# A two-layer hybrid trunk on one core: residual by loading transfers, squares summed by TensorE, weight sums on VectorE, parked tiles loaded ahead

## The chip, the cores and the metric

The kernel runs on one core of one Trainium2 chip. The metric is the device time of one execution in microseconds; lower is better. A time is the median of several runs of one program. A core has TensorE (PE in the profile, with its weight loads listed as PEld), VectorE (DVE), ScalarE (ACT), GpSimd (POOL) and SyncE (SP), which issues most transfers. Each engine takes its own instructions in order; semaphores tie them together.

## The reference

Two residual layers over a stream x of 1024 tokens by 1024 features, all float32. Each layer does

```python
    for layer in range(DEPTH):
        h = rms_norm(x, norm_mix[layer])
        # layer 0: RG-LRU recurrent block; layer 1: forgetting attention
        y_mem = memory_group(xq, mem, norm_mem[layer], w_mem_kv[layer], ...)
        x = x + jnp.concatenate([y_mix, y_mem], axis=-1) @ w_out[layer]
        x = x + sqrelu_mlp(rms_norm(x, norm_mlp[layer]), w_mlp_in[layer], w_mlp_out[layer])
```

with `sqrelu_mlp(h, w1, w2) = square(relu(h @ w1)) @ w2` and a hidden width of 4096. `memory_group` attends from the tokens to 256 normalised memory tokens, whose keys and values are one product with `w_mem_kv`. `rms_norm` needs, for each token, the mean of squares over the 1024 features.

## The kernel before, in words

Everything is kept transposed: features on the 128 partitions, tokens along the row, in tiles of 128 x 512 (one chunk m of 128 features, one half h of the tokens). The SBUF holds 86 such slots, named `f` (float32) or `r` (the rounded type fp32r that TensorE reads); a pool object hands them out and takes them back. A float32 product is made of three fp32r matmuls: each operand is split into `hi` (ScalarE, copy with rounding) and `lo` (VectorE, subtraction), and hi·hi, hi·lo and lo·hi are summed in PSUM. Weights go the same way: SP loads a raw tile `wr` (L307), ScalarE makes `wh` (L311), VectorE makes `wl` (L312; GpSimd for a part of them). The eight PSUM banks carry the names "pj" (2), "s" (2), "pt" (3) and "o" (1).

The order of each engine's instructions is made when the program is built: Python generators emit the work, some of them woven together, and a scheduler that simulates the engines orders what is emitted by its own estimate of times.

The MLP of a layer is cut into eight groups g of 512 hidden features. Each group does a first product `mlp_z` (w1, then relu and square) and a second `mlp_out` (w2). Both use a Strassen-like scheme with seven block products instead of eight (keys b11, b21, t2, t3, t1, t4, b22), so sums of tiles and sums of weight blocks are needed besides. The weight sums of a w1 unit that start from "S2" are seven additions by GpSimd in `_wunit` (L349 twice, L350 twice, L354 at double width, L351 twice), for the w2 units likewise. A `mlp_out` has seven passes of 24 matmuls into four banks; `copies` (ScalarE, L990) takes a bank into a tile at the first half of a sum, `plus` (VectorE, L995) adds a bank to a tile at the second half.

The residual stream x lies in DRAM as `xs` ("xspill" in the profile). Groups 0 to 6 add their results to it with accumulating transfers that GpSimd issues (`send`, L1122). Group 7 does it otherwise: at the key t1 of its `mlp_z`, `acc_load` lets SP load all 16 tiles of `xs`; as a first half comes out, GpSimd adds it to the loaded tile (L1143, 12 per layer); VectorE adds the second half, and `sink` stores the tile, as the output or (layer 0) back to `xs` with squares and splits for the next layer.

The sums of squares for a norm are made by `sqacc`: ScalarE squares a tile (L432), GpSimd adds the square to a running tile `ss` (L438), and `norm_fin_g` lets TensorE sum over partitions with four one-column matmuls against a constant column `cD` (L372), one per 128 tokens.

Two ways of bringing work forward matter here. In the second layer `mlp_park` does the first two products of groups 0, 1 and (in `mlp`, as "wait") 2 early, stores four tiles per group to DRAM ("park"), and `mlp_z` loads them when the group comes (L1044, L1047) and puts two of them into PSUM by a matmul with the identity (L1049). And `kv(l)`, which loads, normalises and projects the memory tokens, is a generator that is advanced from outside: for the second layer at the end of group 7's `mlp_z` of the first, where it loads (L546), splits (L555, L556) and squares; its products (L379) use the banks in `TUNE["kvt"]`, "pj" for the second layer. The output projections are `outproj2` (first layer) and `outproj` (second layer, L894), which add the residual on VectorE (L911, L865) and call `sqacc`.

Of the kernel before, what the change touches and what calls it, by code (L numbers as in the profile page):

```python
# [19 lines left out]
P = 128  # L20
# [57 lines left out]
class Unit:  # L78
# [3 lines left out]
    def __init__(self, src, names, at):  # L82
        self.src, self.names, self.buf = src, names, {}
# [42 lines left out]
def chain(*gs):  # L126
# [5 lines left out]
    "kvt": ('pt', 'pj'),  # L132
# [42 lines left out]
class Builder:  # L175
# [4 lines left out]
    def __init__(self, ctx, tc, ins, out):  # L180
# [36 lines left out]
        self.parked = {}  # L217
        self.xg = [None, None]
# [120 lines left out]
    def _wunit(self, hi, lo, unit, what):  # L339
        G, V = self.nc.gpsimd, self.nc.vector  # L340
# [117 lines left out]
    def norm_fin_g(self, h, bcast, behind=None):  # L458
        nc = self.nc
        ss = self.ss[h]  # L460
        st = self.psum("o")
        for t in range(4):
            self.mm(st[:, t:t + 1], [(ss[:, t * P:(t + 1) * P], self.cD)], behind if t == 0 else None)
# [3 lines left out]
        self.F.put(ss)  # L467
# [73 lines left out]
    def kv(self, l):  # L541
        nc = self.nc
        raw = [self.F.get() for _ in range(4)]
        for i in range(4):
            for j in range(2):
                nc.sync.dma_start(raw[i][:, j * M:(j + 1) * M], self.ins["memT"][2 * i + j])  # L546
        ss = self.F.get()
        xs, rel = [], []
        for i in range(4):
            a, b = self.R.get(), self.R.get()  # L550
            rel += [a, b]
            for j in range(2):
                g = self.pc(f"gmem{l}", 2 * i + j)
                s = slice(j * M, (j + 1) * M)
                nc.scalar.activation(a[:, s], raw[i][:, s], AF.Copy, scale=g)  # L555
# [3 lines left out]
            nc.scalar.activation(sq[:, :H], raw[i][:, :H], AF.Square)  # L559
# [293 lines left out]
    def outproj(self, h, ks, src, dst, gain, last, banks=("pj",)):  # L853
        nc = self.nc
        for m in range(8):
# [10 lines left out]
            if last:  # L866
                self.sqacc(m, h, xv)
# [10 lines left out]
    def outproj2(self, h, k0, k1, src, gain, side):  # L878
# [25 lines left out]
        for m in range(8):  # L904
# [7 lines left out]
            self.sqacc(m, h, xv)  # L912
# [47 lines left out]
    def plan_unit(self, name, i, names=Unit.ALL):  # L960
        src = dict(zip(("a11", "a12", "a21", "a22"), self.ins[name][4 * i:4 * i + 4]))
        u = Unit(src, names, len(self.plan))
        self.plan += [(None, 1024, u, k) for k in names]

    def plan_mlp(self, l, parked, wait):
        for g in wait:
            self.plan_unit("w1", 8 * l + g, Unit.ALL[:2])
        for g in range(8):
            self.plan_unit("w1", 8 * l + g, Unit.ALL[2:] if g in parked + wait else Unit.ALL)
# [27 lines left out]
    def relu2(self, f, src, h):  # L997
        n = slice(0, H)
        self.nc.vector.scalar_tensor_tensor(f[:, n], src, 0.0, self.rsb[h][:, n], ALU.max, ALU.mult)  # L999
        self.nc.scalar.activation(f[:, n], f[:, n], AF.Square)  # L1000

    def mlp_park(self, g):
# [4 lines left out]
        d = self.parked[g] = self.dr.tile([4, P, H], F32, name=self.nm("park"))  # L1007

        def done(o, ps):
            c = self.F.get()  # L1010
            self.nc.sync.dma_start(d[o], t[o][:, n])
            self.nc.vector.tensor_tensor(c[:, n], t[o][:, n], ps, ALU.add)
            self.relu2(c, c[:, n], 0)
            self.nc.sync.dma_start(d[2 + o], c[:, n])
            self.F.put(t[o], c)

        yield from self.product([self.psum("pj") for _ in range(2)], b21, True, done)

    def mlp_z(self, l, g, hook):
# [20 lines left out]
        if g in self.parked:  # L1040
            d = self.parked.pop(g)
            for o in range(2):
                f = self.F.get()
                nc.sync.dma_start(f[:, n], d[o])  # L1044
                t.append(f)
                f = hz[o]["b11"] = self.F.get()
                nc.sync.dma_start(f[:, n], d[2 + o])  # L1047
# [55 lines left out]
    def mlp_out(self, l, g):  # L1103
# [21 lines left out]
        def sink(q, a, b):  # L1125
            f = self.acc.pop((q, a, b))
# [9 lines left out]
        def keep(a, b):  # L1136
            dst = []

            def first(q, ps):
                self.copies(dst)(q, ps)  # L1140
                if g == 7:
                    c = self.acc[(q, a, b)][:, n]
                    G.tensor_tensor(c, c, dst[q][:, n], ALU.add)  # L1143
                    self.F.put(dst[q])

            def then(q, ps):
                if g == 7:
                    self.plus(self.acc[(q, a, b)], ps)
                    sink(q, a, b)
                else:  # L1150
                    self.plus(dst[q], ps)
                    send(dst[q], q, a, b)
# [3 lines left out]
        def end(q, ps):  # L1156
            if g == 7:
                self.plus(self.acc[(q, 0, 1)], ps)
                sink(q, 0, 1)
# [17 lines left out]
    def mlp(self, l, wait, nxt=None):  # L1177
# [3 lines left out]
        def hook(key):  # L1181
# [550 lines left out]
```

## Time and profile before

| | us |
|---|---|
| time, median of 3 runs | 2159.27 |
| lowest and highest run | 2156.13, 2165.36 |
| the profiled execution, its own time | 2165.67 |
| its span in the trace | 2164.0 |
| TensorE busy | 2066.3 (95%) |
| VectorE busy | 1694.2 (78%) |
| ScalarE busy | 1138.6 (53%) |
| GpSimd busy | 936.8 (43%) |

The profile is of one execution. Times of instructions are microseconds from the span's start. A group of instructions has its line, engine, operation, and output <- inputs by the program's names; brackets give idle time of the engine just before and what ended it. Matmuls overlap one another, so that the busy time of TensorE says little about the pace; the number of matmuls in a stretch, divided by its length, says more, and the granted clock (1.00 is full) stands beside it.

The first MLP begins at about 340 us and ends at about 1010; the second runs from about 1500 to the end, with its parked groups 0 to 2 up to about 1700.

### The profile page before, as it was taken

The numbers are of one execution on the slowest core, as the hardware profiler recorded it, in microseconds if no ns is written. First come the engines' busy times: TensorE is split into PE (matmuls) and PEld (weight loads), VectorE is DVE, ScalarE is ACT, GpSimd is POOL, SyncE is SP. The second block draws the span as 40 slices with busy tenths as digits, with TensorE's granted clock in tenths as the row PEclk, the third lists the DMA queues.
The fourth block names the chain that finished last, engine by engine and source line by source line (L and its number), as shares of the span: only waits on it lengthen the run. The fifth ranks groups of instructions, "written<-read, shape, count | busy, mean of one in ns | idle before, by whom it ended". The sixth has DMA issues, their size and how long they took to land.

```text
span 2164.0 us, 29751 instructions
## 1 busy us (share of the span) xinstructions
PE 2066.3 (95%) x10290; PEld 1713.5 (79%) x10290; DVE 1694.2 (78%) x2698; ACT 1138.6 (53%) x2154; POOL 936.8 (43%) x875
## 2 busy tenths in 40 slices
PE   8999997999999999987999999998989999999998
PEld 6898875777778778766998998776767777787786
DVE  8987689886886877878677778778857678768877
ACT  6765645544444544456555647566444444544443
POOL 3213324444444535547342333424463544445445
PEclk9999999999999999998999999999999999999999
DMA  6323352347436446544768446945263474474482
GB/s 204 119 79 107 113 185 73 84 82 156 88 84 140 95 89 129 124 129 166 268 232 288 131 142 219 288 145 169 83 146 98 107 148 89 79 152 93 87 210 78
DMA packets 126103, 297.38 MB, mean 137 GB/s; under 512 B 14144, under 2 KB 16256, under 8 KB 125952
## 3 DMA queue, kind: packets, MB, share of 16 engines
q1 hardware_dynamic: 84480, 211.50, 29.0%
q0 software_dynamic: 41472, 83.97, 21.9%
q8 instruction: 81, 1.33, 0.2%
q14 instruction: 70, 0.57, 0.1%
HBM read 186.27 MB, written 109.15 MB: 137 GB/s over the span
## 4 chain that ended last, share of the span: by engine, by line
PE 45%; DVE 16%; issue 8%; DMA 5%; POOL 3%; ACT 3%; SPq 0%; DVEq 0%; POOLq 0%; ACTq 0%
PE pspt L979 13%; PE pspj L379 10%; PE pss L979 10%; PE pspj L979 7%; DVE wl L312 4%; DVE r L452 3%; DVE f L999 2%; DMA xspill<-f 2%; DVE f L995 1%; PE pso L979 1%; PE pss L1360 1%; PE pspt L1402 1%; DMA wr<-in_w_dram 1%; POOL wr L354 1%; DVE f L1084 1%
## 5 line engine op out<-in xcount | busy, mean ns | idle before, releaser
L312 DVE TENSOR_TENSOR wl<-wr,wh 128x1024 fp32r<-128x1024 f32 (+2 forms) x362 | 446.6, 1244 | 98.7 <-ACT wh L311 96.0
L979 PE MATMUL pspt<-r,wh 128*128 128x512 f32 x1552 | 494.4, 400 | 3.8 <-ACT f L990 2.2
L1122 POOL DMA_DIRECT2D xspill<-f x224 | 292.2, 1990 | 301.2 <-DVE f L995 292.0
L311 ACT ACTIVATE wh<-wr 128x1024 fp32r<-128x1024 f32 (+3 forms) x411 | 305.4, 765 | 122.4 <-PE pss L979 26.7
L979 PEld LDWEIGHTS pspt<-r,wh 128*128 128x128 f32 x1552 | 294.5, 190 | 77.5 <-issue 2.7
L979 PE MATMUL pss<-r,wh 128*128 128x512 f32 x1024 | 328.9, 400 | 14.4 <-DVE r L452 10.9
L452 DVE TENSOR_TENSOR r<-f,r 128x512 fp32r<-128x512 f32 x282 | 240.7, 865 | 113.3 <-DMA xspill<-f 50.5
L979 PE MATMUL pspt<-r,wl 128*128 128x512 f32 x776 | 309.7, 400 | 2.1 <-DVE wl L312 2.1
L379 PE MATMUL pspj<-wh,r 128*128 128x256 f32 (+1 forms) x1408 | 273.0, 288 | 15.8 <-DVE f L995 11.6
L979 PE MATMUL pspj<-r,wh 128*128 128x512 f32 x816 | 264.5, 405 | 12.4 <-DVE f L865 4.6
L979 PEld LDWEIGHTS pss<-r,wh 128*128 128x128 f32 x1024 | 194.0, 190 | 68.8 <-DVE r L452 17.5
L449 ACT ACTIVATE r<-f 128x512 fp32r<-128x512 f32 x282 | 172.6, 626 | 135.0 <-DMA xspill<-f 51.5
L379 PEld LDWEIGHTS pspj<-wh,r 128*128 128x128 f32 x1408 | 223.6, 191 | 18.9 <-issue 11.9
L1000 ACT ACTIVATE f<-f 128x512 f32<-128x512 f32 x128 | 80.9, 632 | 275.0 <-DVE f L999 274.9
L349 POOL TENSOR_TENSOR wr<-wr,wr 128x512 f32<-128x512 f32 x64 | 104.4, 1817 | 266.1 <-DVE wl L312 252.5
L979 PE MATMUL pss<-r,wl 128*128 128x512 f32 x512 | 204.1, 399 | 4.6 <-DVE wl L312 4.6
L379 PE MATMUL pspj<-wl,r 128*128 128x256 f32 (+1 forms) x704 | 201.6, 287 | 1.2 <-DVE wl L312 1.1
L979 PEld LDWEIGHTS pspj<-r,wh 128*128 128x128 f32 x816 | 155.6, 192 | 52.3 <-ACT wh L311 5.4
L379 PE MATMUL pspj<-r,wh 128*128 128x512 f32 x528 | 175.0, 407 | 10.0 <-ACT wh L311 5.7
L979 PEld LDWEIGHTS pspt<-r,wl 128*128 128x128 f32 x776 | 148.7, 192 | 39.4 <-DVE wl L312 3.8
L979 PE MATMUL pspj<-r,wl 128*128 128x512 f32 x408 | 161.3, 401 | 1.0 <-DVE wl L312 0.9
L351 POOL TENSOR_TENSOR wr<-wr,f 128x512 f32<-128x512 f32 x64 | 146.5, 2582 | 14.9 <-issue 14.6
(291 smaller groups left out, 3985.8 us busy)
## 6 DMA issues: line engine op xcount, KB each, us to landing
wr<-in_w_dram SPq DMA_DIRECT2D x134, 512.0 KB, 4.3
xspill<-f POOLq DMA_DIRECT2D x224, 256.0 KB, 6.7
f<-xspill SPq DMA_DIRECT2D x104, 256.0 KB, 5.0
xspill<-f SPq DMA_DIRECT2D x64, 256.0 KB, 3.2
f<-in_xT_dram SPq DMA_DIRECT2D x32, 256.0 KB, 3.4
wr<-in_wkv_dram SPq DMA_DIRECT2D x16, 512.0 KB, 3.6
wr<-in_wina_dram SPq DMA_DIRECT2D x15, 512.0 KB, 3.7
wsp<-wh SPq DMA_DIRECT2D x14, 512.0 KB, 4.7
```

The costliest lines, as they stand in the source:

```text
L311: self.wact = self.nc.scalar.activation(hi, raw, AF.Copy)
L312: eng.tensor_tensor(lo, raw, hi.bitcast(F32), ALU.subtract)
L349: G.tensor_tensor(r["a11"][:, d], r["a11"][:, d], r["a21"][:, d], ALU.subtract)
L351: G.tensor_tensor(r["a12"][:, d], r["a12"][:, d], x, ALU.subtract)
L354: G.tensor_tensor(r["a21"], r["a21"], r["a22"], ALU.add)
L379: self.lastmm = self.nc.tensor.matmul(out, lhsT=a, rhs=b, start=(j == 0), stop=(j == n - 1))
L449: i = self.nc.scalar.activation(hi[:, :n], src, AF.Copy)
L452: self.nc.vector.tensor_tensor(lo[:, :n], src, hi[:, :n].bitcast(F32), ALU.subtract)
L979: self.lastmm = self.nc.tensor.matmul(ps, lhsT=a, rhs=b, start=(start and c == 0 and j == 0), stop=(c == n - 1 and j == 2), skip_group_che ...
L999: self.nc.vector.scalar_tensor_tensor(f[:, n], src, 0.0, self.rsb[h][:, n], ALU.max, ALU.mult)
L1000: self.nc.scalar.activation(f[:, n], f[:, n], AF.Square)
L1122: nc.gpsimd.dma_start(self.xs[2 * q + a, :, b * H:(b + 1) * H], f[:, n], accum_op=ALU.add)
```

## The change

Six things are written otherwise.

1. In group 7, the residual tile is added by a transfer: GpSimd issues an accumulating load from `xs` onto the tile that holds the first half (after the change L1180, 12 per layer). `acc_load` and its 16 loads go; the last four tiles are loaded by SP in the middle of `mlp_out`.
2. In `outproj2` and in the second layer's last `outproj`, `sq_pe` replaces `sqacc`: each square tile goes to TensorE as four one-column matmuls that add up in a bank "o" (after the change L456), held back by two chunks; GpSimd's additions go.
3. The weight sums of group 0's w1 unit are made by VectorE, in both layers (`u.dve`).
4. Parked tiles of group 0 stay in SBUF; those of groups 1 and 2 are stored, and loaded in the middle of the preceding group's `mlp_out` (`mlp_back`), four transfers each.
5. The second layer's memory tokens are loaded from group 7's key t2 on, and split from its key b22 on, ordered behind the last relu square (`lastsq`). Their products use "pt" banks. The norm steps in group 0 come at t2 and t3.
6. The second layer's last `outproj` uses the banks "pj", "s" and "pt" instead of "pj" alone.

```diff
@@ TUNE
-    "kvt": ('pt', 'pj'),
+    "kvt": ('pt', 'pt'),
@@ _wunit
-        G, V = self.nc.gpsimd, self.nc.vector
+        V = self.nc.vector
+        G = V if unit.dve else self.nc.gpsimd
@@ new
+    def sq_pe(self, m, h, xt):
+        sq = self.F.get()
+        self.nc.scalar.activation(sq[:, :H], xt, AF.Square)
+        if m == 0:
+            self.stp[h] = self.psum("o"), []
+        self.stp[h][1].append((m, sq))
+        self.sq_mm(h, 2)
+
+    def sq_mm(self, h, keep):
+        st, todo = self.stp[h]
+        while len(todo) > keep:
+            m, sq = todo.pop(0)
+            for t in range(4):
+                self.nc.tensor.matmul(st[:, t:t + 1], lhsT=sq[:, t * P:(t + 1) * P], rhs=self.cD,
+                                      start=(m == 0 and t == 0), stop=(m == 7), skip_group_check=True)
+            self.F.put(sq)
@@ norm_fin_g
+        if h in self.stp:
+            self.sq_mm(h, 0)
+            st, ss = self.stp.pop(h)[0], None
+        else:
...
@@ kv
                 nc.sync.dma_start(raw[i][:, j * M:(j + 1) * M], self.ins["memT"][2 * i + j])
+        yield
+        behind = self.lastsq if l else None
...
@@ outproj
-                self.sqacc(m, h, xv)
+                (self.sqacc if gain is None else self.sq_pe)(m, h, xv)
@@ outproj2
-            self.sqacc(m, h, xv)
+            self.sq_pe(m, h, xv)
@@ plan_mlp
+            u = self.plan_unit("w1", 8 * l + g, Unit.ALL[2:] if g in parked + wait else Unit.ALL)
+            u.dve = g == 0
@@ new
+    def mlp_back(self, g):
+        if g in self.parked:
+            d = self.parked[g]
+            self.parked[g] = [self.F.get() for _ in range(4)]
+            for i, f in enumerate(self.parked[g]):
+                self.nc.sync.dma_start(f[:, :H], d[i])
@@ mlp_out
-    def acc_load(self):
-        self.acc = {(q, a, b): self.load_x(2 * q + a, b, self.xs)
-                    for a, b in ((0, 0), (1, 0), (1, 1), (0, 1)) for q in range(4)}
...
             def first(q, ps):
                 self.copies(dst)(q, ps)
                 if g == 7:
-                    c = self.acc[(q, a, b)][:, n]
-                    G.tensor_tensor(c, c, dst[q][:, n], ALU.add)
-                    self.F.put(dst[q])
+                    nc.gpsimd.dma_start(dst[q][:, n], self.xs[2 * q + a, :, b * H:(b + 1) * H], accum_op=ALU.add)
...
         yield from run([self.psum(k) for k in more], "b21", True, c11[1], "t3")
+        mid()
         yield from run(A, "t2", False, c21[0], "t1")
         C = [self.psum(k) for k in more]
+        acc = [self.load_x(2 * q, 1, self.xs) for q in range(4)] if g == 7 else None
...
@@ mlp
+        def hook7(key):
+            if key in ("t2", "b22") and nxt is not None:
+                advance(nxt)
...
-            drain(self.mlp_out(l, g))
+            drain(self.mlp_out(l, g, lambda: self.mlp_back(g + 1)))
@@ run
-        drain(self.outproj(1, K_X, self.xs, self.xs, "gmlp1", True))
+        drain(self.outproj(1, K_X, self.xs, self.xs, "gmlp1", True, ("pj", "s", "pt")))
```

How the instructions move, at three places. First GpSimd at the end of the first layer's MLP, before the change (L1143 adds a loaded residual tile and a first half; L438 adds squares for the next norm):

```order
L1143 TENSOR_TENSOR f_829_7854<-f_829_7854,f_875_8102 128x512
...
L438 TENSOR_TENSOR f_880_8127<-f_880_8127,f_889_8171 128x512
L1143 TENSOR_TENSOR f_830_7856<-f_830_7856,f_896_8194 128x512
L1143 TENSOR_TENSOR f_831_7858<-f_831_7858,f_897_8203 128x512
L1143 TENSOR_TENSOR f_832_7860<-f_832_7860,f_898_8212 128x512
```

and after it (L591 adds the squares of the memory tokens, L440 is the former L438):

```order
L591 TENSOR_TENSOR f_834_7956<-f_834_7956,f_845_7988 128x512
L1180 DMA f_856_8064<-xspill 128x512
L1180 DMA f_857_8073<-xspill 128x512
...
L440 TENSOR_TENSOR f_864_8116<-f_864_8116,f_873_8160 128x512
L1180 DMA f_880_8183<-xspill 128x512
L1180 DMA f_881_8192<-xspill 128x512
```

Each of the additions is a transfer now, at the same place in GpSimd's queue, and the memory tokens' squares come ahead of the first four.

Second, VectorE at the entry of the first MLP after the change (L351, L352, L356 and L353 are the weight sums, L313 the `wl` of a weight, L941 and L471 a residual addition and a split of the projection):

```order
L351 TENSOR_TENSOR wr_69<-wr_69,wr_71 128x512 x2
L463 SCALAR_TENSOR_TENSOR r_406_3789<-f_329_3342,par,r_405_3788 128x512
L313 TENSOR_TENSOR wl_76<-wr_70,wh_73 128x1024
L941 TENSOR_TENSOR f_368_3554<-f_368_3554,pspj_3556 128x512
L463 SCALAR_TENSOR_TENSOR r_408_3793<-f_345_3416,par,r_407_3792 128x512
L352 TENSOR_TENSOR f_383_3627<-wr_72,wr_69 128x512
L471 TENSOR_TENSOR r_398_3723<-f_347_3441,r_397_3722 128x512
...
L356 TENSOR_TENSOR wr_71<-wr_71,wr_72 128x1024
...
L353 TENSOR_TENSOR wr_70<-wr_70,f_383_3627 128x512
```

Before, these additions stood in GpSimd's queue, mixed with the last squares; now they stand between VectorE's splits and residual additions.

Third, TensorE in the second layer's last output projection after the change (L381 are the projection's matmuls, L456 the squares' with one column):

```order
L381 MATMUL pspt_15021<-r_1578_14954,wl_77 128x512
L456 MATMUL pso_14978<-cD,f_1581_14976 128x1 x4
L381 MATMUL pspj_15048<-r_1356_13394,wh_75 128x512
L381 MATMUL pspj_15048<-r_1357_13395,wh_75 128x512
L456 MATMUL pso_14978<-cD,f_1584_15000 128x1 x4
L456 MATMUL pso_14978<-cD,f_1591_15035 128x1 x4
L381 MATMUL pspj_15048<-r_1356_13394,wl_78 128x512
```

Before, one set of four such matmuls stood here in all, behind the last addition; now eight sets stand between the projection's matmuls, three of them close together at this place.

More of the change, by code (lines that the diff above doesn't have):

```diff
@@ L217, in __init__ @@
         self.parked = {}
+        self.stp = {}
         self.xg = [None, None]
@@ L459, in norm_fin_g @@
         nc = self.nc
[L460 to L463, printed above, removed]
+        if h in self.stp:
+            self.sq_mm(h, 0)
+            st, ss = self.stp.pop(h)[0], None
+        else:
+            ss = self.ss[h]
+            st = self.psum("o")
+            for t in range(4):
+                self.mm(st[:, t:t + 1], [(ss[:, t * P:(t + 1) * P], self.cD)], behind if t == 0 else None)
         self.vx[h] = self.small(4, f"vx{h}")
@@ L466, in norm_fin_g @@
         self.rs_tok[h] = self.rsqrt(self.vx[h], 4, f"rst{h}")
-        self.F.put(ss)
+        if ss is not None:
+            self.F.put(ss)
         if bcast:
@@ L554, in kv @@
                 s = slice(j * M, (j + 1) * M)
-                nc.scalar.activation(a[:, s], raw[i][:, s], AF.Copy, scale=g)
+                k = nc.scalar.activation(a[:, s], raw[i][:, s], AF.Copy, scale=g)
+                if behind is not None:
+                    self.after(k, behind)
                 nc.vector.scalar_tensor_tensor(b[:, s], raw[i][:, s], g, a[:, s].bitcast(F32), ALU.mult, ALU.subtract)
@@ L558, in kv @@
             sq = ss if i == 0 else self.F.get()
-            nc.scalar.activation(sq[:, :H], raw[i][:, :H], AF.Square)
+            k = nc.scalar.activation(sq[:, :H], raw[i][:, :H], AF.Square)
+            if behind is not None:
+                self.after(k, behind)
             if i:
@@ L963, in plan_unit @@
         self.plan += [(None, 1024, u, k) for k in names]
+        return u
     def plan_mlp(self, l, parked, wait):
@@ L1006, in mlp_park @@
         yield from self.product([self.psum("pj") for _ in range(2)], b11, True, self.copies(t))
-        d = self.parked[g] = self.dr.tile([4, P, H], F32, name=self.nm("park"))
+        kept = []
         def done(o, ps):
             c = self.F.get()
-            self.nc.sync.dma_start(d[o], t[o][:, n])
             self.nc.vector.tensor_tensor(c[:, n], t[o][:, n], ps, ALU.add)
             self.relu2(c, c[:, n], 0)
-            self.nc.sync.dma_start(d[2 + o], c[:, n])
-            self.F.put(t[o], c)
+            kept.append(c)
         yield from self.product([self.psum("pj") for _ in range(2)], b21, True, done)
+        kept = t + kept
+        if g:
+            d = self.dr.tile([4, P, H], F32, name=self.nm("park"))
+            for i, f in enumerate(kept):
+                self.nc.sync.dma_start(d[i], f[:, n])
+            self.F.put(*kept)
+            self.parked[g] = d
+        else:
+            self.parked[g] = kept
+    def mlp_back(self, g):
[4 more added lines that the diff above has]
+                self.nc.sync.dma_start(f[:, :H], d[i])
     def mlp_z(self, l, g, hook):
@@ L1157, in end @@
             if g == 7:
-                self.plus(self.acc[(q, 0, 1)], ps)
-                sink(q, 0, 1)
+                self.plus(acc[q], ps)
+                sink(acc[q], q, 0, 1)
             else:
```

37 lines of the change are left out of this document (13 added, 24 removed).

## The prediction

> **What bounds the kernel now.** I read the page's first section, then a table of windows, then TensorE's list of waits, and last the timeline where the waits lie.
>
> ```profile
> span 2164.0 us, 29751 instructions
> PE 2066.3 (95%) x10290; PEld 1713.5 (79%) x10290; DVE 1694.2 (78%) x2698; ACT 1138.6 (53%) x2154; POOL 936.8 (43%) x875
> ```
>
> TensorE (PE) is busy for 95% of the span, so all that any reordering can return lies in the other 5% and in stretches where it is busy at a lower clock. The next view has one row for each stretch: its bounds and length, the busy time and instruction count of PE, weight loads, VectorE (DVE), ScalarE (ACT) and GpSimd (POOL), TensorE's granted clock, and the DMA share and rate.
>
> ```profile
> 320.00:370.00 50.00, 37.52 (x145) 27.99 (x144) 50.00 (x55) 26.81 (x44) 26.21 (x14) 0.93 0.23 76
> 930.00:1000.00 70.00, 60.03 (x239) 46.38 (x238) 62.64 (x66) 41.50 (x76) 46.92 (x29) 0.95 0.35 118
> 1000.00:1020.00 20.00, 8.38 (x55) 8.19 (x54) 18.62 (x33) 10.46 (x24) 14.65 (x13) 0.66 0.53 180
> 1480.00:1550.00 70.00, 60.90 (x238) 45.63 (x237) 58.89 (x80) 37.91 (x62) 35.82 (x28) 0.90 0.56 180
> 1570.00:1580.00 10.00, 6.77 (x23) 5.13 (x22) 8.15 (x10) 6.07 (x11) 8.64 (x6) 0.83 0.28 64
> 1600.00:1620.00 20.00, 17.44 (x66) 13.10 (x65) 9.67 (x9) 6.02 (x9) 14.59 (x15) 0.91 0.93 174
> 1650.00:1700.00 50.00, 43.01 (x169) 32.46 (x168) 30.61 (x36) 21.19 (x35) 25.26 (x23) 0.93 0.69 150
> 1780.00:1840.00 60.00, 59.58 (x255) 47.45 (x254) 46.65 (x53) 27.93 (x44) 25.24 (x22) 1.00 0.43 91
> 2120.00:2140.00 20.00, 16.36 (x58) 12.42 (x57) 20.00 (x24) 12.02 (x20) 8.64 (x6) 0.83 0.13 52
> ```
>
> The row at 1780 is the calm middle of the second MLP: 255 matmuls in 60 us, 0.235 us each at clock 1.00; a pass of 24 is 5.65 us. Elsewhere the lost time is the length minus 0.235 times the count. Seam 1, entry of the first MLP (320 to 370): 50 − 34.1 = 15.9. Seam 2, its end (930 to 1020): 13.8 + 12.9 = 26.7. Seam 3, entry of the second MLP and its parked groups (four rows from 1480): 14.0 + 4.6 + 4.5 + 10.2 = 33.3. Seam 4, the end of the program: 6.4. Together 82 us lie at the places that the change touches. In 320 to 370 and 2120 to 2140 VectorE is busy for the whole stretch. Two lists of waits name the releasers (total us, times, longest).
>
> ```profile
> PE pspj L379 <- DVE f L995: 11.6, 1, 11.6
> PE pss L979 <- DVE r L452: 10.9, 15, 4.8
> PE pspt L1049 <- DMA f<-park: 6.7, 2, 4.1
> PE pss L979 <- DVE wl L312: 4.6, 1, 4.6
> ...
> ACT r L555 <- DMA f<-in_memT_dram: 8.8, 1, 8.8
> ```
>
> VectorE releases most of it, and parked tiles coming back release 6.7 us.
>
> **The change, part by part. Seam 1: weight sums and squares.** The timeline gives start, length, engine, operation and, in brackets, the idle time before it.
>
> ```profile
> 331.00 0.68 DVE L942 TENSOR_TENSOR f<-f,f 128x512 f32<-128x512 f32 x1
> 332.14 1.92 POOL L438 TENSOR_TENSOR f<-f,f 128x512 f32<-128x512 f32 x1 [5.33 <-ACT f L432]
> 332.81 1.79 DVE L949 SCALAR_TENSOR_TENSOR f<-f,par,f 128x512 f32<-128x512 f32 x1
> ...
> 344.88 5.24 POOL L349 TENSOR_TENSOR wr<-wr,wr 128x512 f32<-128x512 f32 x2 [4.35 <-DVE wl L312]
> 351.75 3.98 POOL L350 TENSOR_TENSOR f<-wr,wr 128x512 f32<-128x512 f32 x2
> 351.84 1.05 PE L372 MATMUL pso<-cD,f 128*128 128x1 f32 x8 [0.70 <-POOL f L438]
> 355.69 2.85 POOL L354 TENSOR_TENSOR wr<-wr,wr 128x1024 f32<-128x1024 f32 x1
> 358.50 3.39 POOL L351 TENSOR_TENSOR wr<-wr,f 128x512 f32<-128x512 f32 x2
> 364.30 0.50 PE L979 MATMUL pss<-r,wl 128*128 128x512 f32 x1 [4.61 <-DVE wl L312]
> ```
>
> A VectorE operation on two SBUF tiles takes 0.68 us at 331.00 and 1.79 beside a GpSimd addition: each GpSimd tensor operation here costs VectorE about 1.1 us. Seven square additions (L438) go: 7 × 1.1 = 7.7. The weight sums of group 0 keep GpSimd at work for 5.24 + 3.98 + 2.85 + 3.39 = 15.5 us; if VectorE does only such operations in it, it loses 15.5 × (1 − 0.68/1.79) = 9.6. On VectorE they cost it six operations of 0.68 and one of double width, 5.4, so 4.2 remain. Relief of VectorE: 11.9. TensorE pays: the row at 351.84 is one set of four one-column matmuls, 1.05 us; eight sets stand where one stood, 7 × 1.05 = 7.35. Net −4.6 if all relief reaches TensorE; I take −4. Bounds: all 15.9 return, −8.5; or only the 4.61 named at 364.30 goes, 7.35 − 4.61 = +3.
>
> The Trainium skill, "SBUF — State Buffer", section "Who interferes with whom", says that a VectorE operation with two SBUF inputs and a GpSimd operation that reads SBUF exclude each other for the whole instruction. By that rule seven additions like the one of 1.92 us would give back up to 13.4 instead of 7.7, and the seam would come to some −9. The row at 332.81 shows 1.1, and I stay with it.
>
> **Seam 2: the residual of the last group, and the early load of the second layer's memory tokens.**
>
> ```profile
> 968.89 0.64 PE L979 MATMUL pss<-r,wh 128*128 128x512 f32 x1 [4.75 <-DVE r L452]
> 985.29 12.80 POOL L1143 TENSOR_TENSOR f<-f,f 128x512 f32<-128x512 f32 x8
> 1013.19 0.55 PE L379 MATMUL pspj<-wh,r 128*128 128x256 f32 x1 [11.62 <-DVE f L995]
> ```
>
> Twelve additions (1.6 us each by the row at 985.29) and 12 of 16 loads go; 12 accumulating transfers come. Contention falls by 12 × 1.1 = 13 us on VectorE, but three square additions of the memory tokens and eight of their splits move into the stretch near 950 that was busy before, which takes back about 3 × 1.1 + 8 × 0.44 = 7 (0.44 is an estimate: half a 0.68 row for half the columns, and start-up). At 1013.19 the memory products wait 11.62 us for a "pj" bank that VectorE frees with its last additions; now they take "pt" banks, which the last pass does not use: freed one pass, 5.65 us, sooner, and VectorE gets there earlier. I take 8 of the 12.9 lost after 1000. ScalarE's 8.8 us on the late memory tokens goes too; it lay behind residual loads on SP's queue. Of the 13.8 lost before 1000 I take 6, the net relief. Seam 2: −14. Bounds: only the bank wait shrinks, −8; nearly all returns, −24.
>
> What the transfers cost is seen from the accumulating stores of groups 0 to 6: the same engine, size and kind, in the other direction (rows: of the page's issues; of one line, min/median/max).
>
> ```profile
> xspill<-f POOLq DMA_DIRECT2D x224, 256.0 KB, 6.7
> L1122 POOL DMA_DIRECT2D xspill<-f x224: 842/1631/4887, 407.5 to 2083.6; - x112
> DMA to landing us min/median/max: 3.7/6.7/12.8
> ```
>
> Issue 1.63 plus landing 6.7 plus VectorE's 0.68 is 9.0 us at the medians. VectorE's addition comes one pass after the copy and TensorE wants the bank another pass later, so 11.3 us are free: hidden. At the maxima it is 18.4, 7 us late; that is a rival below. The last four residual tiles still come through SP, issued three passes ahead: nothing.
>
> **Seam 3: squares, banks and parked tiles.**
>
> ```profile
> 1516.65 1.22 PE L979 MATMUL pspj<-r,wh 128*128 128x512 f32 x2 [4.26 <-DVE f L865]
> 1576.62 1.62 PE L979 MATMUL pspj<-r,wh 128*128 128x512 f32 x3 [3.23 <-ACT wh L311]
> 1609.76 1.10 PE L1049 MATMUL pspt<-f,ident 128*128 128x512 f32 x2 [2.56 <-DMA f<-park]
> ```
>
> The squares pay 7.35 again. Seven additions less and the weight sums moved relieve VectorE by 11.9 as at seam 1; seven banks instead of two let the output projection run while VectorE adds, so the 4.26 at 1516.65 should go. Of the 14.0 lost in 1480 to 1550 I take 10. Parked tiles of groups 1 and 2 are loaded in the preceding group's output passes, five of 5.65 us ahead of use; group 0's are never stored. The 6.7 us of waits go, with a little of the low clock behind them: 7. Net 7.35 − 17 = −10. Bounds: all but 2 returns, −24; only the park waits go, +1.
>
> **Seam 4** is seam 2's residual part without a next layer.
>
> ```profile
> 2122.02 5.09 POOL L1143 TENSOR_TENSOR f<-f,f 128x512 f32<-128x512 f32 x3 [2.98 <-ACT f L990]
> 2128.32 0.50 PE L979 MATMUL pss<-r,wh 128*128 128x512 f32 x1 [3.06 <-DVE r L452]
> ```
>
> Three visible additions slow VectorE just ahead of the 3.06 wait. I take −3 of 6.4, bounds 0 and −6.
>
> Sum: −4 − 14 − 10 − 3 = −31 (bounds −4 and −62). The profiled execution took 2165.67 us for its span of 2164.0, and lies 6.4 above the median 2159.27 of runs from 2156.13 to 2165.36. So 2134.7 for such an execution, and **2128** for the median.
>
> **The rivals.** (A) *VectorE stays the bound.* It is full for all of 320 to 370, takes the sums over, and gets the memory splits where it was late. Then each seam gives its lower end, +3 − 8 + 1 + 0 = −4: 2155. Against it: GpSimd's 15.5 us really leave those stretches. (B) *Nearly all lost time returns*, since stalls feed each other: a stall lowers the clock (0.66 to 0.83 in the windows), and late matmuls delay the next copies. Sum of the upper ends, −62: 2097. Against it: the waits have many releasers, and the change does not touch the weights' splits that end several. (C) *Slower: the squares' matmuls stop TensorE.* They stand in order among the projection's matmuls, and each set needs ScalarE's square of a tile that VectorE has just added. Where VectorE lags by more than the two chunks (11.3 us) that they are held back, all behind them waits. At 16 sets × 4.26 us (the wait on just such an addition, at 1516.65) that is +68, against −31: 2196. It decides from 31/16 = 1.9 us per set. Against it: 4.26 occurred at a lag of no chunks; for it: in the second layer two sets stand next to each other at two places, with less than two chunks ahead. (D) *The accumulating loads are late*: 7 us at the maxima, for two passes in each layer, is 28: 2156. For it: those transfers run where VectorE is busiest; against it: the median fits.
>
> The rule for (D) in the Trainium skill, the same page and section: a transfer issued by GpSimd that looks stalled by VectorE was starved of the port while its descriptors were written. The spread of L1122's issue, 0.84 to 4.89 us, agrees that issuing can stretch; by the rule (D) would be the likelier of the two no-change cases.
>
> **How the numbers follow.** Forecast 0.55 (own range 2112 to 2142), A 0.14, B 0.16, C 0.07, D 0.08. The range 2104 to 2157 leaves out about half of B, C, and the far halves of A and D: 0.2. Half a per cent, about what can be told from no change, is 10.8 us: faster is below 2148.5, slower above 2170. Faster: 0.55 + 0.16 + half of A + a little of D = 0.80. Slower: most of C, 0.06. Same: 0.14.
>
> **What would show it.** Right: the wait for L995 by the memory products falls to under 4 us; no wait for park is left; the lost time in the windows at the four seams falls from 82 to about 50, with sixteen sets of one-column matmuls of about 1.05 us included; VectorE's 512-wide operations near 350 read 0.68. Wrong: waits of several us ahead of the one-column matmuls (C), VectorE additions waiting for the accumulating transfers in the last groups (D), or a VectorE still full at both entries with TensorE waiting for wl (A).

## The result and the profile after

The changed kernel takes 2133.52 us (median of 4 runs, 2129.36 to 2142.39), the kernel before 2158.84 us in the 4 runs that stand with it (2156.13 to 2165.36): a ratio of 0.9884, 95% interval 0.9845 to 0.9922. The forecast was 2128, range 2104 to 2157. The profiled execution of the change took 2132.55 us for a span of 2130.8, 33.1 less than the profiled one of before; the medians differ by 25.3.

The first section of the page after:

```profile
span 2130.8 us, 29902 instructions
PE 2065.7 (97%) x10402; PEld 1716.9 (81%) x10402; DVE 1654.5 (78%) x2712; ACT 1137.0 (53%) x2154; POOL 857.8 (40%) x847
```

TensorE does 112 records more and is busy just as long. Its mean granted clock over the span is 0.989, where it was 0.981. As an estimate from these two, full clock was withheld for 1.9% of 2164.0 us, 41 us, before and for 1.1% of 2130.8, 23 us, after: up to 18 of the 33 us can be time at the low clock that no longer occurs. GpSimd has 79 us less to do.

To say where the time went, I took the start of the same VectorE instruction in two traces and looked at how the difference grows from place to place (us of the change's trace; a positive number is time that the other kernel takes more in that stretch). The first row is what the change saved; the other rows belong to the experiments below.

| stretch | 0–290 | 290–420 seam 1 | 420–860 | 860–1065 seam 2 | 1065–1415 | 1415–1720 seam 3 | 1720–2080 | 2080–end seam 4 |
|---|---|---|---|---|---|---|---|---|
| before | 3.8 | 11.0 | -0.2 | 7.2 | 0.9 | 4.5 | 0.5 | 5.3 |
| forecast of the saving | 0 | 4 | 0 | 14 | 0 | 10 | 0 | 3 |
| u_sq | 2.1 | 1.2 | 0.6 | -0.9 | 1.5 | -1.3 | 0.3 | 0.0 |
| u_s2 | 1.4 | -0.4 | -0.8 | -0.7 | 2.6 | 1.3 | -0.2 | 0.0 |
| u_sq_s2 | 0.8 | 10.3 | -0.3 | 0.3 | 2.1 | -2.2 | -0.3 | 0.0 |
| u_res | 5.5 | -1.1 | -0.5 | 2.3 | 1.6 | 0.4 | 0.2 | 4.3 |
| u_kvt | 0.0 | -1.6 | -0.6 | 0.7 | 0.5 | -3.9 | -0.2 | 0.0 |
| u_kv | 0.0 | -1.3 | -0.2 | -3.7 | 2.5 | -4.6 | -0.1 | 0.1 |
| u_kv_res | 6.9 | -1.2 | -0.5 | 8.2 | 1.1 | -1.5 | 0.0 | 4.4 |
| u_banks | 4.5 | 0.1 | 0.3 | -0.3 | -1.1 | -1.3 | -0.2 | 0.0 |
| u_park | 3.7 | -1.9 | 0.2 | -1.3 | 0.4 | 6.5 | -0.2 | 0.0 |
| k_mid | 6.9 | -2.2 | 0.2 | -1.5 | 3.0 | 1.3 | 0.1 | 0.0 |
| k_lull | 2.0 | -1.6 | 0.3 | -3.2 | 3.5 | -6.8 | 0.1 | 0.1 |
| k_best | 1.0 | -1.7 | -0.3 | -4.1 | 0.7 | -4.8 | -0.2 | 0.0 |

The four seams give 28.0 of the 33.0; the rest came in stretches that the change leaves as they were, and differs from run to run. The rows also show how far one execution can be trusted: where a kernel leaves a stretch as in the change, it still differs by up to 6.9 us before 290, from -2.2 to +0.1 at seam 1, from -1.3 to +0.3 at seam 2, by up to 3.5 between the seams 2 and 3, by nothing to speak of at seam 4, and from -6.8 to +1.3 at seam 3. So a few us at seam 3 mean nothing in one execution.

The table of windows of the change, with the columns of the prediction's:

```profile
320.00:370.00 50.00, 50.00 (x240) 41.17 (x239) 43.26 (x72) 30.26 (x48) 5.55 (x7) 1.00 0.28 90
```
```profile
940.00:950.00 10.00, 5.90 (x22) 3.90 (x22) 10.00 (x18) 8.39 (x15) 4.58 (x5) 0.94 0.64 104
950.00:960.00 10.00, 7.63 (x18) 5.40 (x19) 10.00 (x13) 7.04 (x12) 5.88 (x5) 0.55 0.52 160
...
970.00:980.00 10.00, 9.49 (x42) 7.37 (x41) 3.40 (x6) 2.20 (x5) 2.65 (x5) 1.00 1.07 239
...
990.00:1000.00 10.00, 7.16 (x46) 6.75 (x45) 9.99 (x12) 5.49 (x15) 9.11 (x8) 0.83 0.62 220
```
```profile
1440.00:1480.00 40.00, 36.53 (x174) 29.07 (x174) 26.14 (x62) 22.76 (x53) 11.07 (x18) 0.85 0.34 105
1480.00:1520.00 40.00, 36.86 (x163) 29.38 (x162) 32.91 (x57) 22.58 (x36) 4.50 (x8) 0.90 0.45 135
```

At the entry of the first MLP TensorE is busy for all 50 us at clock 1.00 and VectorE has 7 us to spare, where it had none. At the end of the first layer a hole is left: only 40 matmuls in the 20 us from 940, at a clock of 0.55 in its second half, while VectorE is full. The waits of TensorE, and one of VectorE:

```profile
PE pspj L381 <- ACT wh L312: 7.6, 3, 5.5
PE pspt L1011 <- DVE f L1027: 6.1, 3, 4.2
PE pss L1011 <- DVE r L471: 5.1, 14, 1.2
PE pss L1011 <- ACT f L1022: 4.5, 3, 2.3
...
DVE f L1027 <- DMA f<-xspill: 11.7, 6, 6.0
```

The first row lies in the first 100 us and stood there before (7.4). The waits of 11.6 (memory products for a bank), 6.7 (parked tiles) and 4.6 us (weights' wl) are gone. New is the last row: VectorE waits for the accumulating loads.

### The profile page after: what moved, and what is told of

It reads as the page before. It is cut to its first block, busy times and chain, and to the rows that moved or that the text cites. A ratio compares the mean times of both kernels' runs of the same rounds, so it can differ in the third digit from the quotient of the medians.

```text
span 2130.8 us, 29902 instructions
## 1 busy us (share of the span) xinstructions
PE 2065.7 (97%) x10402; PEld 1716.9 (81%) x10402; DVE 1654.5 (78%) x2712; ACT 1137.0 (53%) x2154; POOL 857.8 (40%) x847
## 4 chain that ended last, share of the span: by engine, by line
PE 55%; DVE 13%; issue 6%; DMA 4%; ACT 1%; POOL 1%; DVEq 0%; SPq 0%; POOLq 0%; ACTq 0%
PE pspt L1011 15%; PE pss L1011 12%; PE pspj L381 10%; PE pspj L1011 8%; DVE wl L313 3%; DVE r L471 3%; DVE f L1031 2%; DMA xspill<-f 2%; PE pso L1011 2%; PE pspt L381 1%; PE pspt L1438 1%; PE pss L1396 1%; DMA f<-xspill 1%; DVE f L1027 1%; DVE f L1130 1%
## 5 line engine op out<-in xcount | busy, mean ns | idle before, releaser
L313 DVE TENSOR_TENSOR wl<-wr,wh 128x1024 fp32r<-128x1024 f32 (+2 forms) x362 | 442.2, 1232 | 112.6 <-ACT wh L312 108.0
L471 DVE TENSOR_TENSOR r<-f,r 128x512 fp32r<-128x512 f32 x282 | 225.0, 808 | 100.3 <-DMA xspill<-f 57.6
L1011 PE MATMUL pspj<-r,wh 128*128 128x512 f32 x816 | 259.3, 397 | 4.1 <-ACT f L1022 1.8
L381 PE MATMUL pspj<-wh,r 128*128 128x256 f32 (+1 forms) x1280 | 246.7, 286 | 3.9 <-ACT wh L312 1.7
L381 PEld LDWEIGHTS pspj<-wh,r 128*128 128x128 f32 x1280 | 200.9, 188 | 7.0 <-ACT wh L312 1.9
L351 POOL TENSOR_TENSOR wr<-wr,wr 128x512 f32<-128x512 f32 x60 | 94.6, 1777 | 271.6 <-DVE wl L313 258.8
L381 PE MATMUL pspj<-wl,r 128*128 128x256 f32 (+1 forms) x640 | 181.5, 284 | 1.2 <-DVE wl L313 1.1
L381 PE MATMUL pspj<-r,wh 128*128 128x512 f32 x488 | 163.7, 411 | 9.6 <-ACT wh L312 5.9
L353 POOL TENSOR_TENSOR wr<-wr,f 128x512 f32<-128x512 f32 x60 | 140.2, 2650 | 17.8 <-issue 17.6
```

Source lines behind the costliest of these rows:

```text
L313: eng.tensor_tensor(lo, raw, hi.bitcast(F32), ALU.subtract)
L351: G.tensor_tensor(r["a11"][:, d], r["a11"][:, d], r["a21"][:, d], ALU.subtract)
L353: G.tensor_tensor(r["a12"][:, d], r["a12"][:, d], x, ALU.subtract)
L381: self.lastmm = self.nc.tensor.matmul(out, lhsT=a, rhs=b, start=(j == 0), stop=(j == n - 1))
L471: self.nc.vector.tensor_tensor(lo[:, :n], src, hi[:, :n].bitcast(F32), ALU.subtract)
L1011: self.lastmm = self.nc.tensor.matmul(ps, lhsT=a, rhs=b, start=(start and c == 0 and j == 0), stop=(c == n - 1 and j == 2), skip_group_che ...
```

## The experiments

Each kernel is the change with a part undone (u_) or moved (k_), by the edit shown. Its stretches are compared with the change's own trace. Except for k_lull and k_best, with four runs each, every figure is of one profiled execution.

**u_sq: squares back on GpSimd.**

```diff
-                (self.sqacc if gain is None else self.sq_pe)(m, h, xv)
+                self.sqacc(m, h, xv)
-            self.sq_pe(m, h, xv)
+            self.sqacc(m, h, xv)
```

> The change with the sums of squares given back to GpSimd in both layers (its other parts kept). Theory 1 (VectorE is the bound at the entries of the MLPs, and a GpSimd tensor operation beside it stretches it by 1.1 us): at the entry of the first MLP VectorE's two-input operations read 1.8 us again beside seven additions (7.7 us), TensorE saves 7 sets x 0.9 = 6.3 us of one-column matmuls, waits for wl of some 2 us return, and the entry comes out 1 to 5 us later. Theory 2 (the one-column matmuls are a plain cost on TensorE and the weight sums alone brought the gain): 6 us sooner at each entry, 12 in all.

Measured: 2136.01 us; seam 1 +1.2, seam 3 -1.3. At seam 1 that is the low end of theory 1, a little above the -2.2 to +0.1 of the kernels that leave it alone; theory 2 falls.

**u_s2: weight sums of group 0 back on GpSimd.**

```diff
-            u.dve = g == 0
```

> The change with the weight sums of group 0 given back to GpSimd in both layers (squares stay on TensorE). Theory 1: 15.5 us of GpSimd additions stretch VectorE by 9.6 where its own sums took 5.4; the wait of 4.6 us for wl that stood at 364.30 before returns at least in part, entry of the first MLP 3 to 6 us later. Theory 2 (the squares alone removed the lag, so the sums have room): within 1 us.

Measured: 2135.68 us; seam 1 -0.4, seam 3 +1.3. Here theory 2 holds. Either part can be taken out at seam 1 for little or nothing.

**u_sq_s2: both edits.**

> The change with both the sums of squares and the weight sums of group 0 given back to GpSimd. By itself either one moved the entry of the first MLP (from 290 to 420 us) by no more than 2 us, where before lost 11.0. Theory 1a (each relieves VectorE enough by itself, so that only both together bring the stall back): 7 to 11 us later there. Theory 3 (neither matters; the norm steps, now at t2 and t3 of group 0, or the order around them did it): within 2 us of the change there.

Measured: 2143.25 us; seam 1 +10.3, of the 11.0 that before lost there. Theory 1a holds, theory 3 (the norm steps) falls. The window from 300 to 360 us, in the change, u_sq, u_s2 and u_sq_s2, in this order:

```profile
300.00:360.00 60.00, 59.67 (x287) 48.49 (x286) 51.64 (x90) 39.18 (x64) 2.38 (x4) 1.00 0.38 123
```
```profile
300.00:360.00 60.00, 54.54 (x212) 41.47 (x211) 55.16 (x84) 36.47 (x59) 13.71 (x11) 0.91 0.38 125
```
```profile
300.00:360.00 60.00, 59.29 (x285) 47.98 (x284) 54.75 (x86) 37.16 (x61) 17.11 (x11) 1.00 0.39 127
```
```profile
300.00:360.00 60.00, 47.66 (x182) 35.48 (x181) 54.94 (x70) 34.13 (x56) 27.49 (x18) 0.89 0.32 110
```

VectorE is about equally busy in the last three, but gets 84, 86 and 70 instructions done: with 27.49 us of GpSimd beside it, it falls behind; with 17.11 (u_s2) it keeps up, and with 13.71 (u_sq) nearly. So the time of GpSimd alone does not order them. In u_sq TensorE has some stalls again and saves the added sets; in u_s2 it pays the sets and has no stall of over 0.7 us. And in u_sq_s2 the wait for wl is back, longer than the 4.61 of before:

```profile
328.48 0.80 PE L924 MATMUL pspj<-r,wl 128*128 128x512 f32 x1 [2.25 <-DVE wl L313]
...
353.29 0.80 PE L1010 MATMUL pspj<-r,wl 128*128 128x512 f32 x1 [6.14 <-DVE wl L313]
```

**u_res: residual of the last group by GpSimd's additions and SP's loads.**

```diff
-                    nc.gpsimd.dma_start(dst[q][:, n], self.xs[2 * q + a, :, b * H:(b + 1) * H], accum_op=ALU.add)
+                    c = self.acc[(q, a, b)][:, n]
+                    G.tensor_tensor(c, c, dst[q][:, n], ALU.add)
+                    self.F.put(dst[q])
+                    dst[q] = self.acc[(q, a, b)]
...
-        acc = [self.load_x(2 * q, 1, self.xs) for q in range(4)] if g == 7 else None
+        acc = [self.acc[(q, 0, 1)] for q in range(4)] if g == 7 else None
@@ hook7
+            if key == "t1":
+                self.acc_load()
```

`acc_load` is the method that the change took out.

> The change with the last group's residual added by GpSimd as before (16 loads by SP, 12 additions per layer). Theory 1 (contention): in the last groups VectorE is stretched by 12 x 1.1 = 13 us; the end of the program comes 3 to 6 us later from the last relu squares on, the end of the first layer 3 to 8 us later. Rival (the accumulating transfers are late as often as the additions stretched VectorE): VectorE's waits of 11.7 us for xspill in the profile of the change go, and the two ends move by less than 1 us.

Measured: 2145.21 us; seam 4 +4.3, seam 2 +2.3. At the end of the program the contention theory holds, and the wait of before is back to the digit:

```profile
2102.71 5.09 POOL L1185 TENSOR_TENSOR f<-f,f 128x512 f32<-128x512 f32 x3 [2.98 <-ACT f L1022]
2103.21 1.78 DVE L471 TENSOR_TENSOR r<-f,r 128x512 fp32r<-128x512 f32 x1
...
2109.01 0.50 PE L1011 MATMUL pss<-r,wh 128*128 128x512 f32 x1 [3.06 <-DVE r L471]
```

Three VectorE operations beside the three additions (L1185) take 1.75 to 1.78 us instead of 0.68, 3.3 us in all, just ahead of that wait.

At seam 2 the +2.3 meets neither theory (3 to 8) nor rival (under 1), and is not far above what one execution can tell.

**u_kvt: memory products on pj again.** The edit is `"kvt": ('pt', 'pj')`.

> The change with the second layer's memory products on the banks pj again. Theory (the bank wait was the loss): TensorE waits again for VectorE's last additions ahead of the memory products, by 5 us or so, since a pass of 5.65 us lies between the two kinds of bank, and the end of the first layer (860 to 1065 us) comes 3 to 6 us later. Rival (the early load and the faster additions removed the wait, whatever the bank): within 1.5 us.

Measured: 2127.42 us; seam 2 +0.7. The wait came back and cost next to nothing:

```profile
989.80 0.55 PE L381 MATMUL pspj<-wh,r 128*128 128x256 f32 x1 [6.41 <-DVE f L1027]
```

With the pt banks the products start sooner, and then wait for wl by 1.06 and 2.55 us at a clock of 0.83 (the window at 990 above): what the bank gave, the weights took. The rival holds as to the time, though not as to the wait.

**u_kv: all of the memory tokens as before** (loads and splits behind the last first product, pj), and **u_kv_res: that and u_res together.**

```diff
-            if key in ("t2", "b22") and nxt is not None:
-                advance(nxt)
+            return
@@ mlp
                     self.pool_parts = TUNE["pb0"]
+                    advance(nxt, 2)
@@ kv
-        behind = self.lastsq if l else None
+        behind = None
@@ TUNE
-    "kvt": ('pt', 'pt'),
+    "kvt": ('pt', 'pj'),
```

> The change with the memory tokens as before (loads and splits behind the last first product, products on pj), the residual by accumulating transfers kept. Theory (the parts at this seam cover for one another, as the squares and the weight sums did): 1 to 3 us longer from 860 to 1065 us. Rival (they add up): 4 to 5 us.

> The change with all that it does at the end of the first layer undone: residual by GpSimd's additions and SP's loads, memory tokens loaded and split behind the last first product, their products on the banks pj. Theory: the end of the first layer (860 to 1065 us) is 6 to 8 us longer, all that before lost there (7.2), though the residual alone brought back 2 to 3 and the banks alone about 1. Rival (the norm steps and other parts matter there): at most 4 us.

Measured: u_kv 2125.21 us, seam 2 -3.7; u_kv_res 2149.88 us, seam 2 +8.2, as its theory had it (6 to 8). Neither theory nor rival for u_kv expected a gain. Together they say that at seam 2 the residual transfers give 11.9 without the new order of the memory tokens (8.2 + 3.7) and 2.3 with it, and that the new order gives 5.9 without the transfers (8.2 - 2.3) and costs 3.7 with them. The bank wait in u_kv_res and in u_kv shows who shortened it:

```profile
1003.90 0.55 PE L381 MATMUL pspj<-wh,r 128*128 128x256 f32 x1 [11.61 <-DVE f L1027]
```
```profile
985.73 0.55 PE L381 MATMUL pspj<-wh,r 128*128 128x256 f32 x1 [5.41 <-DVE f L1027]
```

The transfers took 6.2 us off it, with the bank and the memory tokens' loads as before.

**k_mid: the splits of the memory tokens in the middle of the output passes.** The edit drops "b22" from `hook7` and passes `lambda: advance(nxt)` as `mid` for group 7.

> The change with the second layer's memory tokens split, squared and added not from key b22 of group 7's first product but in the middle of its output passes. Theory 1: the eight splits took VectorE 7.6 us at 934 to 942, where TensorE then waited 4.18 us at 951.62 and ran at clock 0.55 to 960; with them later that wait goes, and the end of the first layer comes 4 to 8 us sooner. Rival (the wait at 951.62 has another cause, or the splits only delay the memory products in its place): within 2 us.

Measured: 2140.22 us; seam 2 -1.5, the rival. The scheduler put the splits 14 us later, and VectorE was still full. In the change, and in k_mid:

```profile
934.40 5.51 DVE L584 SCALAR_TENSOR_TENSOR r<-f,par,r 128x256 fp32r<-128x256 f32 x4
...
936.72 4.33 POOL L591 TENSOR_TENSOR f<-f,f 128x512 f32<-128x512 f32 x3
...
940.44 2.08 DVE L584 SCALAR_TENSOR_TENSOR r<-f,par,r 128x256 fp32r<-128x256 f32 x4
...
951.62 0.77 PE L1011 MATMUL pspt<-r,wh 128*128 128x512 f32 x1 [4.18 <-DVE f L1027]
```
```profile
948.26 5.45 DVE L584 SCALAR_TENSOR_TENSOR r<-f,par,r 128x256 fp32r<-128x256 f32 x4
...
957.98 0.80 PE L1011 MATMUL pss<-r,wh 128*128 128x512 f32 x1 [5.25 <-DVE r L471]
```

In both kernels four splits take 5.5 us beside GpSimd's additions: in the change two weight sums (L353, from 934.01) and then the same tokens' squares (L591), in k_mid those squares. The other four take 2.08 in the change, where the last L591 still runs, and 1.69 in k_mid.

**k_lull: the splits behind ScalarE's copies of the fourth output pass**, where VectorE has room (970 to 980 in the windows above).

```diff
@@ mlp_out
+        late()
         yield from run(A, "t1", False, c22[1], "b22")
@@ copies
-            self.nc.scalar.activation(f[:, :H], ps, AF.Copy)
+            self.lastcopy = self.nc.scalar.activation(f[:, :H], ps, AF.Copy)
@@ kv
-        behind = self.lastsq if l else None
+        behind = self.lastcopy if l else None
```

Here `late` advances `nxt` in group 7, and "b22" is dropped from `hook7` as in k_mid.

> The change with the memory tokens' splits, squares and additions put behind ScalarE's copies of the output passes' fourth pass, where VectorE was busy for only 3.4 of 10 us (970 to 980 in the profile of the change); loads as in the change. Put only into the middle of the output passes they stayed in the full stretch, and TensorE's wait was 5.25 us instead of 4.18. Theory: the splits read 0.4 us each, the waits of 4 to 5 us near 950 fall under 2, and 860 to 1065 us is 4 to 8 us shorter. Rival (VectorE's weight splits and relu work fill that stretch by themselves, or the memory products now wait): within 2 us.

Measured: median 2123.07 us of 4 runs (2121.38 to 2126.90), ratio to before 0.9815, interval 0.9793 to 0.9836, below that of the change (0.9845 to 0.9922) without overlap: the fastest median of the kernels run. Its profile has seam 2 at -3.2, between the rival's 2 and the theory's 4, and -6.8 at seam 3, where it changes nothing. The hole near 950 is gone, four of the splits take 1.66 us while GpSimd issues transfers (the other four 2.14), and the next wait shows:

```profile
961.72 1.66 DVE L584 SCALAR_TENSOR_TENSOR r<-f,par,r 128x256 fp32r<-128x256 f32 x4
...
972.01 0.69 DVE L1027 TENSOR_TENSOR f<-f,pss 128x512 f32<-128x512 f32 x1 [8.63 <-DMA f<-xspill]
...
972.75 1.22 PE L1011 MATMUL pss<-r,wh 128*128 128x512 f32 x2 [4.13 <-DVE f L1027]
```

Now the accumulating loads are what TensorE waits for: rival D, which the crowd on VectorE had covered.

**u_banks: the last output projection on pj alone.** The edit takes `("pj", "s", "pt")` out of the call.

> The change with the second layer's last output projection on the two pj banks again. Theory (TensorE waited for a bank that VectorE frees): a wait of 2 to 4 us for the residual addition returns near 1500, and the stretch from 1415 to 1720 us is 2 to 6 us longer. Rival (relief of VectorE alone removed that wait): within 1.5 us.

Measured: 2134.50 us; seam 3 -1.3, the rival. No wait for the residual addition returns near 1500. A stall stands at another place, longer than any that the change has there, and seam 3 is no longer for it:

```profile
1560.31 1.19 PE L1011 MATMUL pspt<-r,wh 128*128 128x512 f32 x2 [8.02 <-DVE f L1027]
```

**u_park: parked tiles loaded when their group begins.** `mlp_z` calls `mlp_back(g)` itself for g > 0, and `mid` does nothing.

> The change with the parked tiles of groups 1 and 2 loaded only when their group begins, as before; group 0's stay in SBUF. Theory: the waits for parked tiles, 2.6 and 4.1 us before, return, with the low clock behind them: 1415 to 1720 us is 5 to 8 us longer. Rival (the loads were late only because other transfers and stalls stood ahead of them): under 2 us.

Measured: 2139.96 us; seam 3 +6.5, of which 7.7 lie between 1580 and 1720 us, where the kernels that leave seam 3 alone differ by about -2 to +2 (u_banks by +4). As expected, though the wait has another name: ScalarE waits for the parked tiles (25.5 us before, not at all in the change), and TensorE for ScalarE.

```profile
ACT r L468 <- DMA f<-park: 26.4, 4, 10.3
```
```profile
1675.46 0.88 PE L1011 MATMUL pss<-r,wh 128*128 128x512 f32 x2 [3.64 <-ACT f L1022]
```

**k_best: k_lull with the second layer's squares on GpSimd.** The edit is the first of u_sq's two.

> The kernel before this one (memory tokens' splits moved behind the fourth output pass) with the second layer's sums of squares given back to GpSimd; the first layer keeps them on TensorE. The seven added sets cost TensorE 7 x 0.9 = 6.3 us there, and with both layers given back the stretch from 1415 to 1720 us was 1.3 us shorter than in the change. Theory (in the second layer the relief of VectorE does not reach TensorE, so the sets are nearly a plain cost): 1 to 6 us shorter there than in the kernel before this one, 2118 to 2122 us in all. Rival (they pay for themselves as in the first layer): 0 to 4 us longer.

Measured: median 2125.44 us (2123.04 to 2129.33), ratio to before 0.9837, interval 0.9820 to 0.9855: not to be told from k_lull. Seam 3 is 2.0 longer than k_lull's and 4.8 shorter than the change's; within what that stretch does by itself. The sets are saved, and a wait that k_lull does not have stands there instead:

```profile
1501.13 0.79 PE L1011 MATMUL pss<-r,wh 128*128 128x512 f32 x1 [6.36 <-DVE r L471]
```

With -1.3 for u_sq and +2.0 here, the squares on TensorE are worth about nothing in the second layer; whether it is a little more or less stays open. Despite its label this kernel is not the fastest.

## Why the prediction was right, and where it was not

The sum was right, -31 for the profiled execution against -28.0 at the seams, and the median 2133.5 lies 5.5 above the forecast. That the sum came so near is luck: seams 1 and 4 gave 9.3 us more than their terms, seams 2 and 3 gave 12.3 less. The direction and the main cause, GpSimd's operations slowing VectorE, were right and are shown by the experiments at seams 1, 2 and 4.

**Seam 1, -4 forecast, -11.0 measured, beyond its bound of -8.5.** The mechanism (VectorE slowed by GpSimd) was right: VectorE's operations read 0.68 again, and the sums cost it about what was forecast (5.4).

```profile
333.15 1.28 DVE L351 TENSOR_TENSOR wr<-wr,wr 128x512 f32<-128x512 f32 x2
...
334.39 0.95 PE L456 MATMUL pso<-cD,f 128*128 128x1 f32 x8
...
339.88 1.22 DVE L356 TENSOR_TENSOR wr<-wr,wr 128x1024 f32<-128x1024 f32 x1
...
346.90 1.39 PE L456 MATMUL pso<-cD,f 128*128 128x1 f32 x12
```

The term mis-sized is "Relief of VectorE: 11.9" carried one for one to TensorE, with 7.35 paid. Two things are wrong in it. The sets are cheaper: 12 records take 1.39, so a set of 8 takes some 0.9 us and seven 6.3. And relief is not a sum: u_sq, u_s2 and u_sq_s2 (1.2, -0.4, 10.3) show that what counts is whether VectorE keeps up; once it does, the whole 15.9 of lost time returns, and more relief gives next to nothing. 15.9 - 6.3 is 9.6; 1.4 stays unaccounted.

**Seam 2, -14 forecast, -7.2 measured; just outside its bounds (-8 to -24).** The residual's part was right: 13 us of contention forecast, 11.9 measured by itself (u_kv against u_kv_res). What the memory tokens' work costs VectorE was forecast about right too, 3 × 1.1 + 8 × 0.44 = 7 against 5.51 + 2.08 = 7.6, the delays by GpSimd within it. Two steps failed. The first is "of the 13.8 lost before 1000 I take 6, the net relief": the 7 us landed where VectorE was fullest, TensorE waited 4.18 us and then ran at a clock of 0.55, so that relief and load did not simply offset each other. u_kv shows that the new order as a whole costs 3.7 beside the transfers, and k_lull that another place for the splits returns 3.2. The second is "8 of the 12.9", put down to the bank and to an earlier VectorE: the bank was worth 0.7 (u_kvt), the transfers shortened the wait (11.61 to 5.41), and with the pt banks waits for wl took its place. (The 12.9 does not follow from the prediction's rule, by which 20 - 0.235 × 55 is 7.1. But 43 of those 55 matmuls have half the columns, so the rule counts too little, and the wait of 11.62 alone is more.)

**Seam 3, -10 forecast, -4.5 measured, inside its bounds.** The parked tiles were near: 7 forecast, 6.5 measured for those of groups 1 and 2. "Of the 14.0 lost in 1480 to 1550 I take 10", against 7.35 paid, failed: all but the parked tiles together cost 2.0 in that execution. Undoing squares, weight sums or banks alone moves the seam by -1.3, +1.3 and -1.3, and squares and sums together by -2.2. The waits moved instead of going, and part of the sets ran at half pace there:

```profile
1470.04 1.86 PE L456 MATMUL pso<-cD,f 128*128 128x1 f32 x8
...
1488.13 0.95 PE L456 MATMUL pso<-cD,f 128*128 128x1 f32 x8
...
1506.15 1.22 PE L1011 MATMUL pss<-r,wh 128*128 128x512 f32 x2 [2.35 <-ACT r L468]
```

Why this stretch varies by 8 us among kernels that leave it alone is known in part only. In the 20 us from 1460 on the change has a clock of 0.69. In the same place k_lull has 0.83 and u_kv 0.91, both behind the same wait of 2.06 us, and they come through it 1.1 and 4.9 us sooner. Why the clock differs is open, and so is the rest.

**Seam 4, -3 forecast, -5.3 measured, inside its bounds.** u_res brings 4.3 back. The prediction took half of the 6.4 lost and gave no reason for the half; as at seam 1, nearly all returned.

**The rivals.** A (VectorE stays the bound) is true for seam 2 alone, and there by the memory tokens. B (nearly all returns) is true of seams 1 and 4. C (one-column matmuls stop TensorE) did not happen: of the sixteen sets one waited, for 0.5 us, the ones close together in the second layer included. D (late transfers) happened on VectorE, 11.7 us of waits, at most 5.99, but reached TensorE in the change with only 0.51 and 1.00; in k_lull with 4.13. Its sum counts the issue twice: the profile's landing times run from the issue on, so the 9.0 us at the medians should read 7.4.

**The signs.** Three of the signs named for being right came: VectorE's 512-wide operations near 350 read 0.68, the memory products no longer wait for VectorE's last additions, and no engine waits for a parked tile to come back. The fourth nearly did: with 28.0 us returned, 54 of the 82 are left, where about 50 were named. One of those named for being wrong came too, VectorE's waits for the accumulating loads.

## What to carry to other kernels

Where an engine falls behind, count whether it keeps up after the edit, not how many us are taken off it: two reliefs of one engine in one stretch can be worth little more than the first alone, as at seam 1, and then undoing only one of them shows almost nothing. Before moving work into a stretch, look at the windows for the engine it lands on, and at what moves with it. A trace compared instruction by instruction tells edits at different seams apart in one execution each, if the stretches that were left alone are used to see how much differs by itself.

## What the runs showed of the hardware

The accumulating loads are late through landing, not through issuing. In the change, the eight of the third and fourth passes:

```profile
964.04 7.07 POOL L1180 DMA_DIRECT2D f<-xspill  x8 [4.35 <-ACT f L1022]
...
977.24 0.69 DVE L1027 TENSOR_TENSOR f<-f,pss 128x512 f32<-128x512 f32 x1 [5.99 <-DMA f<-xspill]
```

They are issued in 7.07 us, one per 0.88 us, near the least that a single one takes (0.86). Taken one by one (the rows that begin at 964.04, 967.11 and 969.34), the first, the fifth and the last take this long from issue to landing:

```profile
DMA to landing us min/median/max: 4.0/4.0/4.0
```
```profile
DMA to landing us min/median/max: 10.0/10.0/10.0
```
```profile
DMA to landing us min/median/max: 11.7/11.7/11.7
```

The wait of 5.99 that ends at 977.24 is for the fifth, the first load of the fourth pass (967.11 + 10.0). The DMA engines' share is 1.07 in that stretch. At the end of the program VectorE waits for four such loads in turn and goes on at 2115.52, 2116.82, 2118.08 and 2119.38: they land one behind another, some 1.3 us apart. The Trainium skill ("SBUF — State Buffer", "Who interferes with whom") puts a transfer that looks stalled by VectorE down to GpSimd being kept from the port while it writes descriptors; these eight were issued at 0.88 us each and do not bear that out. Single issue rows grow from 0.88 to 2.06 us as they follow one another, so a spread like that of L1122 in the prediction need not mean port trouble either.

The same section has the second of two contending instructions wait for the whole of the first. The rows of the change agree:

```profile
934.01 1.30 POOL L353 TENSOR_TENSOR wr<-wr,f 128x512 f32<-128x512 f32 x1 [1.22 <-issue]
934.40 1.20 DVE L584 SCALAR_TENSOR_TENSOR r<-f,par,r 128x256 fp32r<-128x256 f32 x1
935.27 1.49 POOL L353 TENSOR_TENSOR wr<-wr,f 128x512 f32<-128x512 f32 x1
935.52 1.52 DVE L584 SCALAR_TENSOR_TENSOR r<-f,par,r 128x256 fp32r<-128x256 f32 x1
```

Each split begins beside a GpSimd addition and ends some 0.3 us after it (935.60 after 935.31, 937.04 after 936.76); four take 5.51 us so, and 1.66 where GpSimd only issues transfers. The second to begin can be GpSimd as well. Before the change three VectorE splits ran at full speed beside one weight sum, and it was the sum that took longer, 3.53 us where the second of the pair (at 348.37) took 1.74:

```profile
344.88 3.53 POOL L349 TENSOR_TENSOR wr<-wr,wr 128x512 f32<-128x512 f32 x1 [4.35 <-DVE wl L312]
345.39 1.88 DVE L452 TENSOR_TENSOR r<-f,r 128x512 fp32r<-128x512 f32 x3
```

So the 1.1 us that the prediction read at 332.81 is about what was left of one addition when VectorE came to it (the operation ends at 334.60, the addition at 334.06), and no fixed price: in these rows the loss lies between nothing and most of an addition. That row does not speak against the rule, as the prediction took it to. The -9 that it worked out by the rule lies nearer to the -11.0 of seam 1 than its -4, though seam 1 also shows that relief does not simply add up.
